# An unused tile of 416 bytes at the high end of SBUF

## The chip, the core and the metric

The kernel runs on one core of a Trainium2 chip. The metric is the device time of one execution in microseconds (us). The core has five engines with an instruction stream each: TensorE (PE in the profile, its weight loads PEld), VectorE (DVE), ScalarE (ACT), GpSimd (POOL) and SyncE (SP, which here issues most of the transfers), and 16 DMA engines. SBUF is the memory that the engines read their operands from: 128 partitions, and a tile has an address within the partition.

## The reference

A decoder trunk of two layers on one sequence of 1024 tokens, width 1024, 16 heads of 64, in float32:

```
layer 0: x = x + nsa_attention(rmsnorm(x))      # compressed, selected (top 8 blocks of 64) and window branch, gated
         x = x + swiglu(rmsnorm(x))             # (silu(a) * b) @ w_down, hidden width 2816
shared K/V = rmsnorm(x) @ kv_w                  # three dilation groups
layer 1: x = x + dilated_attention(rmsnorm(x))  # own queries, windows (128,1), (512,4), (2048,16)
         x = x + swiglu(rmsnorm(x))
return rmsnorm(x)
```

A table of 32 relative-position buckets x 16 heads is added to every attention logit.

## The kernel before

All of it is one function, `trunk`, which opens pools of tiles as it goes. A pool is opened on the left (low) or on the right (high) end of SBUF, and tiles of the two ends grow towards each other, so that a pool can be closed while one on the other end stays. The order of all instructions is fixed when the program is built; a tile that takes the memory of an earlier one waits until the earlier one's readers and writers are done.

**Products in three parts.** A float32 operand is split into a high part of type fp32r and the rest (`split`, L134 to L142; `Pairs`, L761 and L762: ACT copies the high part `ph`, DVE subtracts it and leaves `pl`). A product is then three matmuls (`mm3`, L165 to L167). The first operand is the stationary one, loaded as weights; the second moves through:

```
nc.tensor.matmul(ps, lh, rh, start=first, stop=False, ...)     # L165: high x high
nc.tensor.matmul(ps, lh, rl, start=False, stop=False, ...)     # L166: high x low
return nc.tensor.matmul(ps, ll, rh, start=False, stop=last, ...)  # L167: low x high
```

In the profile's names, `dx<-pl,ph` is a matmul into the bank dx with one operand from pl and one from ph; dx<-ph has both from ph tiles.

**The stages** of the profiled execution, in us from its start:

- 0 to 288: the projections of layer 0. The normalized, transposed stream (tiles hH, hL) and the weights (wraw, wh, wl) are all tiles of the right end; the bank is mm.
- 288 to 755: the attention of layer 0. Its pools are on the left, only its output oT on the right. SP loads the bias tiles T (L554) and the tiles K and V; POOL copies a part of each T into C (L561).
- 755 to 1505: output projection and FFN of layer 0.
- 1505 to 1927: K, V and the queries of layer 1, 18 groups of 128 output columns by the same routine as the FFN's first half.
- 1927 to 2245: the attention of layer 1.
- 2245 to 3036: output projection and FFN of layer 1.

**The big products** are by the scheme of seven block products in place of eight. `cols_steps` makes the hidden blocks (and the K, V and query blocks): its second operands are prepared once and kept for the stage, the tiles B11, B21, B22 and T1 to T4, and each of its seven steps is twelve matmuls of 128x512 with the weight's pair (ph, pl), sliced in four, as the stationary operand:

```
def blk(b, a, name, first, prev=None):
    for i in range(4):
        mm = mm3(b, part(a, i), ops[name][i], first and i == 0, i == 3, True)
```

Its banks are ux and uy (in the projections of layer 1 also dr). `rows_steps` makes the FFN's second half and the output projection; both its operands are pairs from one pool:

```
a, b = ready[i]
mm3(banks[t], part(a, t), b, i == 0 and onX != 2, i == n - 1, onX)
```

Its banks are dx and dr, and DVE adds them to the stream xr (L820). An FFN has 22 hidden blocks (`hidden`, each seven steps of `cols_steps`); after two of them come the seven steps of `rows_steps` (`down_steps`, 84 matmuls), put between the next two blocks' steps. So one period is 2 x 84 + 84 matmuls. The raw weights come into slices of the large tile oT (layer 0) or oTb (layer 1), and POOL multiplies them by the norm's gains (L1081).

**Where the tiles lie.** In the FFN of layer 0 the pairs ph, pl and the tiles wd, ta and tb are on the left, the B and T tiles, xr and oT on the right. In the projections of layer 1 the B and T tiles are on the right and the pairs on the left. In the FFN of layer 1 the pairs, wd, ta and tb are on the right, the B and T tiles, xr and oTb on the left. All these tiles have sizes that are multiples of 512 bytes. In the built program the right-hand ones begin at 480 modulo 512 bytes, the left-hand ones of the FFNs and of layer 1's projections at 64.

Of the kernel before, what the change touches and what calls it, by code (L numbers as in the profile page):

```python
# [10 lines left out]
F32 = mybir.dt.float32  # L11
# [80 lines left out]
def trunk(ctx, tc, I, out):  # L92
    nc = tc.nc

    def pool(c, name, side="left", space=None):
        if space is not None:
            return c.enter_context(tc.tile_pool(name=name, bufs=1, space=space,
                                                **({} if space is DR else {"reuse_waits": "tile"})))
        return c.enter_context(tc.tile_pool(name=name, bufs=1, side=side, reuse_waits="tile"))
# [17 lines left out]
        return psum[name].tile([128, 512], F32, name=name, bufs=BANKS.get(name, 1))  # L117

    cst = pool(ctx, "cst")

    ident = cst.tile([128, 128], F32, name="ident")
    nc.gpsimd.dma_start(ident, I["ident"])
# [1541 lines left out]
```

## Time and profile before

| | |
|---|---|
| median of 3 runs | 3033.9 us (3033.78 to 3038.08) |
| profiled execution, span | 3035.7 us |
| TensorE's mean granted clock | 0.983 |
| busy: PE, PEld | 2899.3 us, 2381.4 us |
| busy: DVE, ACT, POOL | 2401.7 us, 1603.6 us, 1630.1 us |
| moved by DMA | 293.43 MB |

The profile is of one execution. Busy times count instructions that do work; a matmul's record has a start, and an end that is modelled and overlaps the start of the next matmul, so the pace of matmuls is read from one start to the next. "The chain" is the work that ended last, followed back from the end of the program to whatever released each step. In a group's line the numbers behind the bar are its busy time in us, the mean of one in ns, and the idle time of the engine just before its instructions with what ended it. A window's line gives each engine's busy time and number of instructions, then the clock granted to TensorE, the mean busy share of the DMA engines and the GB/s.

### The profile page before, as it was taken

To read this page: it belongs to the slowest core of one execution; us is meant where nothing else is said; L and a number is where in the kernel's file an instruction comes from. 1 tells how busy PE (TensorE), PEld (TensorE's weight loads), DVE (VectorE), ACT (ScalarE), POOL (GpSimd) and SP (SyncE) were. 2 spreads that over 40 slices of the span, in tenths; PEclk is the share of its full clock that TensorE was granted. 3 is DMA by queue.
4 is the path that set the end of the run, shared out by engine and by line. 5 is a ranking of instruction groups with operands and counts; after the bars stand their busy time and mean duration, and the time that the engine had idled before them with its cause. 6 is when DMAs were issued, how large, how long until landed. Compare 5 with 4: busy or idle time off the path is not lost.

```text
span 3035.7 us, 44147 instructions
## 1 busy us (share of the span) xinstructions
PE 2899.3 (96%) x14670; PEld 2381.4 (78%) x14670; DVE 2401.7 (79%) x4832; ACT 1603.6 (53%) x3596; POOL 1630.1 (54%) x1751
## 2 busy tenths in 40 slices
PE   7999999999889999999999999899988899999997
PEld 6987888888677877777777778788866787777776
DVE  4432888988988888888876677589899788888887
ACT  5432888887463333333364444689965433333334
POOL 2134666666766555555556787333357755555551
PEclk9999999999999999999999999999999999999999
DMA  6765032121112222222124555876420211112111
GB/s 167 223 191 165 25 103 78 36 56 70 60 53 63 63 67 74 65 59 70 56 95 141 160 160 145 264 209 179 138 94 25 66 55 57 56 46 62 51 45 73
DMA packets 266196, 293.43 MB, mean 97 GB/s; under 512 B 17971, under 2 KB 209347, under 8 KB 265968
## 3 DMA queue, kind: packets, MB, share of 16 engines
q1 hardware_dynamic: 246320, 230.45, 26.3%
q0 software_dynamic: 19648, 60.16, 6.6%
q8 instruction: 116, 1.90, 0.3%
q14 instruction: 112, 0.92, 0.1%
HBM read 227.44 MB, written 78.81 MB: 101 GB/s over the span
## 4 chain that ended last, share of the span: by engine, by line
PE 68%; DVE 16%; ACT 5%; issue 4%; DMA 4%; POOL 2%; SPq 1%; DVEq 0%; ACTq 0%; POOLq 0%
PE ux L165 5%; PE ux L166 5%; PE ux L167 5%; PE uy L166 4%; PE uy L165 4%; PE uy L167 4%; DVE pl L762 4%; PE pt L275 4%; PE dx L166 3%; PE dr L165 3%; PE dx L167 3%; PE dx L165 3%; PE dr L166 3%; PE dr L167 3%; PE mm L165 3%
## 5 line engine op out<-in xcount | busy, mean ns | idle before, releaser
L762 DVE TENSOR_TENSOR pl<-oT,ph 128x512 fp32r<-128x512 f32 x315 | 325.2, 1052 | 41.3 <-ACT ph L761 35.4
L761 ACT ACTIVATE ph<-oT 128x512 fp32r<-128x512 f32 x329 | 199.0, 626 | 228.1 <-PE ux L166 65.8
L275 PE MATMUL pt<-ident,P 128*128 128x128 f32 x1536 | 245.1, 278 | 11.0 <-ACT P L1458 2.7
L761 ACT ACTIVATE ph<-oTb 128x512 fp32r<-128x512 f32 x239 | 143.2, 625 | 189.4 <-PE ux L166 55.7
L762 DVE TENSOR_TENSOR pl<-oTb,ph 128x512 fp32r<-128x512 f32 x229 | 224.4, 1005 | 23.5 <-ACT ph L761 23.4
L820 DVE TENSOR_TENSOR xr<-xr,dr 128x512 f32<-128x512 f32 x336 | 214.6, 679 | 33.9 <-PE dr L167 33.8
L139 DVE TENSOR_TENSOR tl<-pt,th 128x512 fp32r<-128x512 f32 (+1 forms) x320 | 207.1, 651 | 33.8 <-ACT th L138 31.9
L820 DVE TENSOR_TENSOR xr<-xr,dx 128x512 f32<-128x512 f32 x352 | 220.3, 678 | 3.6 <-PE dx L167 2.4
L166 PE MATMUL dx<-pl,ph 128*128 128x512 f32 x512 | 203.4, 401 | 9.7 <-DVE pl L762 9.0
L688 POOL TENSOR_SCALAR P<-P,sm,gates 128x384 f32<-128x384 f32 (+7 forms) x256 | 183.5, 728 | 53.4 <-DVE sm L686 48.0
L275 PEld LDWEIGHTS pt<-ident,P 128*128 128x128 f32 x1536 | 179.8, 142 | 30.0 <-ACT P L1458 6.7
L138 ACT ACTIVATE th<-pt 128x512 fp32r<-128x512 f32 (+1 forms) x320 | 177.2, 563 | 44.3 <-PE pt L275 40.4
L167 PE MATMUL dx<-ph,pl 128*128 128x512 f32 x512 | 200.0, 397 | 0.3 <-DVE pl L762 0.3
L684 ACT ACTIVATE P<-P,m 128x384 f32<-128x384 f32 (+7 forms) x256 | 170.7, 669 | 16.1 <-DVE m L682 8.4
L1081 POOL TENSOR_TENSOR oT<-oT,gffn 128x512 f32<-128x512 f32 x92 | 105.9, 1158 | 136.2 <-DMA oT<-in_ffn_w_up_dram 110.5
L165 PE MATMUL dx<-ph 128*128 128x512 f32 x512 | 157.3, 400 | 6.7 <-DVE xr L820 3.3
L1081 POOL TENSOR_TENSOR oTb<-oTb,gffn 128x512 f32<-128x512 f32 x92 | 106.4, 1165 | 99.1 <-DMA oTb<-in_ffn_w_up_dram 77.0
L298 PE MATMUL o<-tl,V 128*128 128x256 f32 x540 | 148.8, 299 | 7.4 <-POOL tl L291 3.7
L297 PE MATMUL o<-th,V 128*128 128x256 f32 x540 | 151.4, 296 | 2.7 <-ACT th L138 1.4
L290 POOL TENSOR_SCALAR th<-traw 128x128 fp32r<-128x128 f32 (+1 forms) x112 | 75.1, 674 | 129.3 <-ACT traw L289 47.7
L1458 ACT ACTIVATE P<-P,st 128x384 f32<-128x384 f32 (+2 forms) x256 | 139.6, 547 | 7.6 <-PE pt L1569 4.1
L166 PEld LDWEIGHTS dx<-pl,ph 128*128 128x128 f32 x512 | 97.6, 191 | 39.5 <-DVE pl L762 19.4
(617 smaller groups left out, 9582.4 us busy)
## 6 DMA issues: line engine op xcount, KB each, us to landing
qB<-xr POOLq DMA_DIRECT2D x96, 256.0 KB, 4.7
oT<-in_ffn_w_up_dram SPq DMA_DIRECT2D x92, 256.0 KB, 3.0
oTb<-in_ffn_w_up_dram SPq DMA_DIRECT2D x92, 256.0 KB, 3.0
Q<-qB SPq DMA_DIRECT2D x40, 512.0 KB, 7.0
wd<-in_ffn_w_down_dram SPq DMA_DIRECT2D x66, 256.0 KB, 2.6
oT<-in_b_w_q_dram SPq DMA_DIRECT2D x48, 256.0 KB, 3.5
K<-kBs SPq DMA_DIRECT2D x40, 256.0 KB, 9.5
wraw<-in_a_w_in_dram SPq DMA_DIRECT2D x18, 512.0 KB, 4.9
```

Source lines behind the costliest of these rows:

```text
L138: nc.scalar.activation(H_, src, AF.Copy)
L139: nc.vector.tensor_sub(L_, src, f32(H_))
L165: nc.tensor.matmul(ps, lh, rh, start=first, stop=False, skip_group_check=bool(shared))
L166: nc.tensor.matmul(ps, lh, rl, start=False, stop=False, skip_group_check=bool(shared))
L167: return nc.tensor.matmul(ps, ll, rh, start=False, stop=last, skip_group_check=bool(shared))
L275: nc.tensor.transpose(ps[:, i * 128:(i + 1) * 128], b, ident)
L684: nc.scalar.activation(P[:, e, :n], P[:, e, :n], AF.Exp, bias=mm[:, e:e + 1], scale=-1.0, accum_out=sm[:, e:e + 1])
L688: nc.gpsimd.tensor_scalar(P[:, e, :n], P[:, e, :n], sm[:, e:e + 1], gt(g, t, br, 2 * hp + e, 1), op0=OP.mult, op1=OP.mult)
L761: nc.scalar.activation(h, src, AF.Copy)
L762: (eng or nc.vector).tensor_sub(l, src, f32(h))
L820: nc.vector.tensor_add(xs, xs, banks[t])
L1081: nc.gpsimd.tensor_mul(v, v, gains[:, k:k + 4].unsqueeze(2).to_broadcast([128, 4, 128]))
```

## The change

A pool named "shift" is opened on the right, ahead of all others of that end, and one tile of 128 partitions x 104 floats (416 bytes in each partition) is taken from it. No instruction uses the tile.

```
     cst = pool(ctx, "cst")
+    pool(ctx, "shift", "right").tile([128, 104], F32, name="shift")
```

All 1114 tiles of the right end begin 416 bytes lower, at 64 modulo 512 bytes in place of 480; those of the left end stay. Every engine has the same instructions in the same order. What differs, beside addresses, is some waits at the places where a tile takes memory that others have left, since a shifted tile may overlap other ones than before. Lines below L119 have numbers higher by one, and tile numbers are higher by four.

The waits that differ are nearly all on SP where the attention of layer 0 begins (286 to 297 us). T8 to T11 are the first bias tiles for the first half of the tokens, K2, K3 and V2 the first keys and values; what the wait names is the semaphore (DMASW and DMAHW are transfers that POOL and SP have issued). Before:

```order
L554 DMA T8_2725<-sA_74 128x512 [waits DMAHW0_49]
L554 DMA T9_2732<-sA_74 128x512 [waits DMASW7_49,DMAHW1_49,DMASW0_49,DVE_49]
L554 DMA T10_2739<-sA_74 128x512 [waits DMASW4_49,DMAHW2_49,DMASW3_49,DVE_49]
L554 DMA T11_2746<-sA_74 128x512 [waits DMAHW3_49,DMASW2_49,DMASW1_49]
L267 DMA K2_2753<-kS_79 64x1024 [waits DMAHW4_49,DMASW6_49,DMASW5_49]
L268 DMA K2_2753<-kS_79 64x1024 [waits DMAHW5_49]
L569 DMA K3_2754<-kS_79 64x1024 [waits DMAHW6_49,PE_49]
L570 DMA K3_2754<-bS_81 16x1024 [waits DMAHW7_49]
L580 DMA V2_2759<-vS_80 128x4x128 [waits DMAHW0_49]
```

The same rows of SP after the change:

```order
L555 DMA T8_2729<-sA_78 128x512 [waits DMAHW0_49]
L555 DMA T9_2736<-sA_78 128x512 [waits DMASW4_49,DMASW7_49,DMASW3_49,DMAHW1_49,DMASW0_49,DVE_49]
L555 DMA T10_2743<-sA_78 128x512 [waits DMAHW2_49,DMASW2_49,DMASW1_49]
L555 DMA T11_2750<-sA_78 128x512 [waits DMAHW3_49,DMASW6_49,DMASW5_49]
L268 DMA K2_2757<-kS_83 64x1024 [waits DMAHW4_49]
L269 DMA K2_2757<-kS_83 64x1024 [waits DMAHW5_49]
L570 DMA K3_2758<-kS_83 64x1024 [waits DMAHW6_49,PE_49]
L571 DMA K3_2758<-bS_85 16x1024 [waits DMAHW7_49]
L581 DMA V2_2763<-vS_84 128x4x128 [waits DMAHW0_49,PE_49]
```

Each wait for POOL's stores has moved to the load one place ahead: T9 also waits for the two that T10 waited for, T10 for T11's, T11 for K2's, and K2 for none; V2 has a wait for a matmul of the stage before. In the attention of layer 1 one wait for PE has moved from the load of T126 to the one ahead of it, T125.

## The prediction

> **What bounds the kernel now.** I read the page first: the line of engines (the fraction of the span that each is busy) and the head of the chain that ended last (which engine's work, followed back from the end, fills the span).
>
> ```profile
> span 3035.7 us, 44147 instructions
> PE 2899.3 (96%) x14670; PEld 2381.4 (78%) x14670; DVE 2401.7 (79%) x4832; ACT 1603.6 (53%) x3596; POOL 1630.1 (54%) x1751
> PE 68%; DVE 16%; ACT 5%; issue 4%; DMA 4%; POOL 2%; SPq 1%; DVEq 0%; ACTq 0%; POOLq 0%
> ```
>
> TensorE (PE) is the bound, in busy time and in the chain. An average over stages can mislead, so next come stretches of single stages: the last projections of layer 0 (212 to 287), the FFN of layer 0 (900 to 1350), the K/V and query projections of layer 1 (1600 to 1905, and a part of them, 1816 to 1918), and the FFN of layer 1 (2400 to 2960).
>
> ```profile
> core 0: us, PE busy (x) PEld busy (x) DVE busy (x) ACT busy (x) POOL busy (x), PEclk, DMA share, GB/s
> 212.00:287.00 75.00, 75.00 (x332) 62.09 (x331) 12.81 (x18) 9.78 (x16) 33.57 (x72) 1.00 0.68 201
> 900.00:1350.00 450.00, 447.71 (x1909) 357.01 (x1908) 387.47 (x524) 168.11 (x289) 252.75 (x189) 1.00 0.26 68
> 1600.00:1905.00 305.00, 301.35 (x1296) 240.39 (x1295) 209.93 (x220) 142.15 (x223) 220.97 (x242) 1.00 0.52 151
> 1816.00:1918.00 102.00, 102.00 (x437) 81.97 (x436) 66.56 (x71) 47.17 (x71) 63.70 (x73) 1.00 0.57 169
> 2400.00:2960.00 560.00, 557.98 (x2375) 443.54 (x2374) 481.25 (x655) 207.32 (x356) 303.95 (x230) 1.00 0.18 53
> ```
>
> PE is full in all of them at a granted clock of 1.00, but the matmuls do not all come at one pace. 75 us hold some 331 of them, 226 to 227 ns each; 102 us hold some 436, 234 ns each. All are 128x512 fp32r matmuls. That asks for the timeline of PE, where two starts in a row give the pace.
>
> ```profile
> 211.96 0.39 PE L167 MATMUL mm<-hH,wl 128*128 128x512 f32 x1
> ...
> 287.47 0.39 PE L167 MATMUL mm<-hH,wl 128*128 128x512 f32 x1
> ...
> 1004.65 0.39 PE L166 MATMUL dx<-pl,ph 128*128 128x512 f32 x1
> ...
> 1006.23 0.39 PE L167 MATMUL dx<-ph,pl 128*128 128x512 f32 x1
> 1006.46 0.40 PE L165 MATMUL uy<-B21h,ph 128*128 128x512 f32 x1
> ...
> 1008.80 0.39 PE L166 MATMUL uy<-B21l,ph 128*128 128x512 f32 x1
> ...
> 1815.62 0.39 PE L166 MATMUL dr<-T1l,ph 128*128 128x512 f32 x1
> ...
> 1918.71 0.40 PE L167 MATMUL uy<-T3h,pl 128*128 128x512 f32 x1
> ```
>
> From 211.96 to 287.47 lie 333 steps without a gap: 75.51 / 333 = 226.8 ns. From 1815.62 to 1918.71 lie 440: 103.09 / 440 = 234.3 ns. In one stretch of the FFN, with the same neighbours on the other engines, the eight steps from 1004.65 to 1006.46 take 1.81 us (226 ns) and the ten from 1006.46 to 1008.80 take 2.34 us (234 ns). What divides them is where the two operands lie. hH, hL, wh and wl are all tiles of the right end, and in dx<-ph,pl both operands come from the pair tiles of one pool. In uy<-B21h,ph and dr<-T1l,ph the B and T tiles come from one end of SBUF and the pair tiles ph, pl from the other. In the built program the right-hand tiles begin at 480 modulo 512 bytes, the left-hand ones of these stages at 64. So, in this trace, a matmul whose stationary and moving operand begin at the same place modulo 512 runs at 226.8 ns when undisturbed, and one whose operands do not takes 7.5 ns more. No other difference that I tried (distance in bytes, side, layer, number of matmuls into one bank) sorts the groups.
>
> **The change, part by part.** (1) The unused tile itself: no instruction reads or writes it, every engine has the same instructions in the same order, so it costs 0. (2) The tiles of the right end move by 416 bytes, from 480 to 64 modulo 512, where the left ones of the dense stages lie. Which matmuls does that change from mixed to same? Those of `cols_steps`, seven steps of 12 matmuls: 22 x 84 = 1848 in each FFN, twice, and 18 x 84 = 1512 in the projections of layer 1; 5208 in all. The dx and dr matmuls, and the projections of layer 0, have both operands on one side and stay alike.
>
> What one is worth: the undisturbed ends give 234.3 - 226.8 = 7.5 ns. In the busy loop of an FFN I take less. Over both FFN stages, averaging steps under 320 ns in the timeline, ux and uy stand at 233.8 ns, dx, already alike, at 229.4 and dr at 231, since there the other engines are busy too (DVE 387.47 of 450 us). After the change I expect ux and uy to run as dx and dr do, nearest to dx, which also accumulates in a held bank: 233.8 - 229.4 = 4.4 ns. How much of it reaches the end shows in the loop's period, one recurring piece of the chain of waits in each FFN:
>
> ```profile
> 1184.94 2.39 DVE xr L820 x4
> 1244.20 2.39 DVE xr L820 x4
> ...
> 2615.36 2.39 DVE xr L820 x4
> 2674.63 2.39 DVE xr L820 x4
> 2733.95 2.39 DVE xr L820 x4
> ```
>
> A period of two hidden blocks is 59.3 us (1244.20 - 1184.94; 2674.63 - 2615.36) and holds 252 matmuls: 168 x 233.8 + 84 x 230 ns = 58.6 us, so PE accounts for all but 0.7 us of it. Hence 168 x 4.4 = 0.74 us less per period, 58.5 after, and 22 x 0.74 = 16.3 us in both layers. In the projections of layer 1 DVE is busy 66.56 of 102 us, between the clean stretch (12.81 of 75) and the FFN; I take 228 ns after, 234.3 - 228 = 6.3 ns x 1512 = 9.5 us. Sum 25.8 us of PE's time. PE is idle 2.3 of 450, 2.0 of 560 and 3.7 of 305 us in these stretches, so nearly all of it lies on the path; I let 90% through, as ends of steps wait for DVE and transfers: 23 us.
> Bounds: 5208 x 7.5 ns = 39 us if all reach 226.8, at 92% 36 us; below, dr's 231 in the FFN, 3696 x 2.8 = 10.3, with the projections at 231 also, 1512 x 3.3 = 5.0, and 60% through: 9 us.
>
> A rule of the Trainium skill speaks against this: "SBUF — State Buffer", section "Who interferes with whom", gives PE two independent read ports, one for the moving operand and one for the weight load, and says that PE never waits on anyone. By it the place of an operand would be no matter and the sum 0. The 226.8 and 234.3 ns of this trace do not fit that, unless something else parts them; that is the first rival.
>
> (3) Waits that change, since tiles now take memory that other tiles left: at the start of layer 0's attention SP's bias loads T9 and T10 wait for a store that T10 and T11 waited for before, and a load of K moves ahead. SP and POOL there:
>
> ```profile
> 286.58 6.69 SPq L554 DMA_DIRECT2D T<-sA  x3
> 293.70 0.71 SPq L267 DMA_DIRECT2D K<-kS  x1
> ...
> 301.90 0.51 POOL L558 TENSOR_SCALAR_AFFINE_SELECT TW<-T 128x384 f32<-128x384 f32 x1
> 302.35 0.23 POOL L561 COPY C<-T 128x32 f32<-128x32 f32 x1
> 302.70 0.40 POOL L561 COPY C<-T 128x32 f32<-128x32 f32 x2
> 303.71 0.23 POOL L561 COPY C<-T 128x32 f32<-128x32 f32 x1
> ...
> T<-sA SPq DMA_DIRECT2D x32, 256.0 KB, 4.4
> ```
>
> The whole queue is through with T by 293.3, at the latest the time for T9; it lands at the median of 4.4 us by 297.7, and its copy comes at 302.70. What hides it is the first attention blocks' own work: 5 us in hand. Were the landing 10 us, 0.6 us would be lost. Behind T9 stand only K and V on SP, needed later still. Cost 0. In layer 1, one T load takes a PE wait from the next one that is over 20 us old: 0.
> (4) Matmuls of 128x256 in the attentions, o<-th,V above all: layer 0's are left-side on both operands and stay; in layer 1 some 384 have operands on both sides, at unlike places before and after. The 256-wide matmuls of the first stages start 117 to 120 ns apart, the alike ones no faster than the others: 384 x 3 ns, about 1 us of either sign; I take 0.
> (5) DVE, ACT, POOL and transfers: do they feel the place?
>
> ```profile
> oT<-in_ffn_w_up_dram SPq DMA_DIRECT2D x92, 256.0 KB, 3.0
> oTb<-in_ffn_w_up_dram SPq DMA_DIRECT2D x92, 256.0 KB, 3.0
> L762 DVE TENSOR_TENSOR pl<-oT,ph 128x512 fp32r<-128x512 f32 x315 | 325.2, 1052 | 41.3 <-ACT ph L761 35.4
> L762 DVE TENSOR_TENSOR pl<-wd,ph 128x512 fp32r<-128x512 f32 x86 | 78.9, 919 | 3.1 <-ACT ph L761 3.1
> L762 DVE TENSOR_TENSOR pl<-tb,ph 128x512 fp32r<-128x512 f32 x56 | 69.1, 1234 | 40.3 <-ACT ph L761 40.3
> L762 DVE TENSOR_TENSOR pl<-ta,ph 128x512 fp32r<-128x512 f32 x56 | 55.2, 985 | 12.7 <-ACT ph L761 12.6
> ```
>
> A weight load lands in 3.0 us on either side. pl<-oT,ph reads tiles of both ends, pl from wd, ta and tb those of one end: 919, 985 and 1234 ns lie around the 1052. Place does not order them, and I take 0.
>
> The profiled execution took 3035.7 us, 1.8 above the median of 3033.9; the saving is the same against either. 3033.9 - 23 = 3011 us.
>
> **The rivals.** (a) *The place is not the cause.* cols_steps differs from the others in more than its sides: it always streams a prepared block past four slices of a pair. Then every matmul keeps its pace and the time stays 3034. For it speaks only that I have no stretch of cols_steps with both operands on one side; against it, that dx<-pl,ph has the same slices and the same banks' length of accumulation.
> (b) *DVE takes over.* It is busy 387.47 of 450 us, 51 of each period of 59.3. At a period of 58.5 it stands at 87%, so it is no bound by sum, but a pair pl that comes late stops PE. If half of the 25.8 us comes back so, 13 us remain: 3021.
> (c) *Slower: DVE's two SBUF reads collide.* Now oT or oTb lies like ph and pl. If those 544 operations (315 + 229) went from about 1032 to the 1234 ns of pl<-tb, +20%, and PE gained nothing, it would cost what they hold of the chain: pl's share there is
>
> ```profile
> by line: PE ux L165 5.5%; PE ux L166 5.4%; PE ux L167 5.3%; PE uy L166 4.3%; PE uy L165 4.3%; PE uy L167 4.3%; DVE pl L762 4.1%; issue 4.0%; PE pt L275 3.8%; PE dx L166 3.0%; PE dr L165 2.8%; PE dx L167 2.8%; PE dx L165 2.8%; PE dr L166 2.7
> ```
>
> 4.1% or 124 us, two thirds of it theirs, 83 us x 20% = 16 us: 3050. With PE's gain of 23 us it decides from +28% on. Against it: wd at 919 and ta at 985 already lie so.
>
> **How the numbers follow.** Forecast (2999 to 3017 us) 0.69; (b), 3017 to 3028, 0.13; (a) 0.12; (c) 0.06. The range 2999 to 3028 takes in the first two. A measurement of this kernel can tell some 0.2%, 6 us (the three runs lie 4.3 us apart), so: faster 0.82, same 0.12, slower 0.06.
>
> **What would show it.** In the changed profile the run of matmuls that now goes from 1815.62 to 1918.71 has steps near 228 ns instead of 234.3; the period of the FFN falls from 59.3 to about 58.5 us; the steps at 211.96 to 287.47 stay at 226.8; DVE's mean for pl<-oT stays near 1052; POOL's first copy of T does not wait. The forecast is wrong if ux and uy keep 234 ns (a), or go to 227 while the period stays (b).

## The result, and the profile after

The changed kernel takes 3015.0 us (median of 6 runs, 3012.0 to 3022.8) against 3038.7 us for the kernel before, run beside it (6 runs, 3033.8 to 3046.4): a ratio of 0.9924 with a 95% interval of 0.9908 to 0.9939. That is 23 us of 3034. 3011 were forecast, 23 us below the 3033.9 of the page before. The profiled execution took 3014.1 us, its span is 3012.3.

The head of the page, and the engines' shares of the chain that ended last:

```profile
span 3012.3 us, 44147 instructions
PE 2869.0 (95%) x14670; PEld 2378.2 (79%) x14670; DVE 2405.6 (80%) x4832; ACT 1600.7 (53%) x3596; POOL 1640.1 (54%) x1751
PE 61%; DVE 22%; ACT 6%; issue 5%; DMA 3%; POOL 2%; SPq 1%; DVEq 0%; ACTq 0%; POOLq 0%
```

PE's busy time fell by 30 us, the other engines' hardly moved. In the chain PE went from 68 to 61% and DVE from 16 to 22%: PE still bounds, but DVE is now last more often. In PE's timeline, the same matmuls as in the prediction (dx into uy<-B21, and the start of the run that was 1815.62 to 1918.71 before):

```profile
998.80 0.39 PE L168 MATMUL dx<-ph,pl 128*128 128x512 f32 x1
...
999.93 0.39 PE L166 MATMUL uy<-B21h,ph 128*128 128x512 f32 x1
...
1002.20 0.39 PE L167 MATMUL uy<-B21l,ph 128*128 128x512 f32 x1
...
1802.00 0.39 PE L167 MATMUL dr<-T1l,ph 128*128 128x512 f32 x1
...
1903.60 0.39 PE L168 MATMUL uy<-T3h,pl 128*128 128x512 f32 x1
```

The five steps up to 999.93 take 1.13 us (226 ns), the ten after it 2.27 us (227 ns, 234 before): the step in pace between dx and uy is gone. The long run takes 101.60 us in place of 103.09. 440 steps at 226.7 ns would be 99.7 us; the rest is six longer steps, the longest 1.1 us, which were not there before.

Both traces hold the same 14670 matmuls in the same order, so they can be laid on each other. I split the steps from one start to the next into pace (under 320 ns in both) and gaps (the others), and take the differences by stage (755 to 1505, 1505 to 1927 and from 2245 on in the trace before; matmuls of other widths count in the last two columns only):

```
                          pace of the 512-wide    gaps     all steps of the stage
FFN and output, layer 0        -14.0 us         +6.8 us          -7.0 us
projections of layer 1          -9.8            +7.1             -3.3
FFN and output, layer 1        -14.6            +5.3             -9.1
elsewhere                       -0.1            -2.5             -3.7
sum                            -38.5           +16.6            -23.1
```

So the pace gave 38 us, and 16 to 17 of these came back as gaps. In the projections of layer 1 the gaps of different executions differ by as much: three later kernels in which little pace was won there, or none, had 5.1, 7.7 and -0.4 us more gaps than the profile before. What was lost there is not put down to the change. The 12 us in the two FFNs are: other profiles with the full pace and all of DVE's work (416 bytes on the left, 160 bytes, the changed kernel once more, all below) have 9.5, 13.5 and 15.1 us more gaps there than before, and that with 32 bytes, at a fifth of the pace gain, 3.0. The stretch of one FFN in the windows, and a recurring piece of the chain in each FFN, which give the period:

```profile
core 0: us, PE busy (x) PEld busy (x) DVE busy (x) ACT busy (x) POOL busy (x), PEclk, DMA share, GB/s
900.00:1350.00 450.00, 445.96 (x1934) 360.67 (x1933) 397.50 (x531) 169.52 (x292) 256.18 (x188) 1.00 0.26 67
...
1222.81 2.98 DVE pl L763 x2
1280.93 2.61 DVE pl L763 x2
...
2586.13 2.98 DVE pl L763 x2
2702.41 2.99 DVE pl L763 x2
2818.67 2.99 DVE pl L763 x2
```

The period is 58.1 us in both (1280.93 - 1222.81; 2702.41 - 2586.13 is two of them): 58.5 was forecast from 59.3, and 252 matmuls at 227 ns alone would be 57.2. PE's idle time in the stretch rose from 2.3 to 4.0 us, and DVE's share from 86 to 88%.

The moved waits of SP, and DVE's subtractions:

```profile
290.95 2.35 SPq L555 DMA_DIRECT2D T<-sA  x3
...
301.83 0.41 POOL L562 COPY C<-T 128x32 f32<-128x32 f32 x2
...
L763 DVE TENSOR_TENSOR pl<-oT,ph 128x512 fp32r<-128x512 f32 x315 | 333.7, 1079 | 40.8 <-ACT ph L762 34.6
```

T9 is issued at 290.95 in place of 286.58, its copy comes at 301.83 without an idle time ahead of it: hidden. pl<-oT, whose operands now begin at one place, takes 1079 ns, 1052 before. The subtractions from ta and tb, whose operands began at one place before as well, went from 985 to 1096 and from 1234 to 1118 ns, so a few per cent here say nothing of the place.

### The profile page after: what moved, and what is told of

It reads as the page before. It is cut to its first block, busy times and chain, and to the rows that moved or that the text cites. A ratio compares the mean times of both kernels' runs of the same rounds, so it can differ in the third digit from the quotient of the medians.

```text
span 3012.3 us, 44147 instructions
## 1 busy us (share of the span) xinstructions
PE 2869.0 (95%) x14670; PEld 2378.2 (79%) x14670; DVE 2405.6 (80%) x4832; ACT 1600.7 (53%) x3596; POOL 1640.1 (54%) x1751
## 4 chain that ended last, share of the span: by engine, by line
PE 61%; DVE 22%; ACT 6%; issue 5%; DMA 3%; POOL 2%; SPq 1%; DVEq 0%; ACTq 0%; POOLq 0%
DVE pl L763 7%; PE ux L166 5%; DVE xr L821 5%; PE ux L167 5%; PE ux L168 4%; PE pt L276 4%; PE uy L166 4%; PE uy L167 4%; PE uy L168 4%; PE dx L167 3%; PE mm L166 3%; PE dx L168 3%; PE mm L167 3%; PE mm L168 2%; PE dr L166 2%
## 5 line engine op out<-in xcount | busy, mean ns | idle before, releaser
L763 DVE TENSOR_TENSOR pl<-oT,ph 128x512 fp32r<-128x512 f32 x315 | 333.7, 1079 | 40.8 <-ACT ph L762 34.6
L762 ACT ACTIVATE ph<-oT 128x512 fp32r<-128x512 f32 x329 | 198.8, 626 | 222.3 <-PE ux L167 58.5
```

The lines of the kernel that those rows point to most:

```text
L762: nc.scalar.activation(h, src, AF.Copy)
L763: (eng or nc.vector).tensor_sub(l, src, f32(h))
```

## The experiments

There were three theories at first. Theory 1: the pace of a matmul is set by how its two operands' places differ. Theory 2: 480 is a bad place by itself, being no multiple of 64. Theory 3: the gain came from the moved waits (beside the seven on SP that are listed with the change, six on POOL differ). The ratios below are to the kernel before, run beside each.

**Another size of the unused tile, 32 bytes.**

```
+    pool(ctx, "shift", "right").tile([128, 8], F32, name="shift")
```

> The unused tile has 32 bytes in place of 416: the right-hand tiles begin at 448 modulo 512, a multiple of 64 as the left-hand 64 is, but not at the same place. Theory 1 (the pace of a matmul is set by the difference of its two operands' places modulo 512): ux and uy keep some 234 ns from start to start, the dr and dx right behind them 228 to 232, and the time stays within 0.2% of before. Theory 2 (what hurts is that 480 is no multiple of 64, and 416 bytes mend that): ux and uy go to 227 ns and the time falls by 0.8%, as with 416 bytes. Theory 3 (the gain of 416 bytes came from moved waits): any time, with ux and uy at 234 ns.

Measured: 0.998 (0.9968 to 0.9992), 6 us less. The pace gain was 7.3 us in all, with ux and uy at 232.8 ns in the FFNs: a small gain and not the 38 us of 416 bytes. All waits of this program are those of the kernel before.

**The unused tile at the other end.**

```
+    pool(ctx, "shift").tile([128, 104], F32, name="shift")
```

> The unused tile of 416 bytes is taken from the left end instead: the tiles of both ends begin at 480 modulo 512, the same place, and no multiple of 64; the right-hand tiles stay where they were before. Theory 1 (difference of the operands' places): ux, uy, dx and dr all at 227 ns, the time 0.6 to 0.9% below before. Theory 2 (480 is a bad place, being no multiple of 64): ux and uy at 234 ns or more, and the time the same as before or above it. Theory 3 (moved waits): the waits of this kernel are others than those of the change, so no gain, at 234 ns.

Measured: 0.9928 (0.9911 to 0.9944), as the change itself. The ten steps of uy<-B21 in PE's timeline, of the kernel with 32 bytes on the right:

```profile
1003.35 0.40 PE L166 MATMUL uy<-B21h,ph 128*128 128x512 f32 x1
...
1005.68 0.40 PE L167 MATMUL uy<-B21l,ph 128*128 128x512 f32 x1
```

and of the kernel with 416 bytes on the left:

```profile
1001.09 0.39 PE L166 MATMUL uy<-B21h,ph 128*128 128x512 f32 x1
...
1003.36 0.39 PE L167 MATMUL uy<-B21l,ph 128*128 128x512 f32 x1
```

The ten steps take 2.33 us against 2.27 us: 233 and 227 ns. With all places multiples of 64 but different the pace is slow; with all at 480 and alike it is fast. Theory 2 falls. Theory 3 isn't tested by this run, against what I had expected of it: since the two ends move towards each other by the same 416 bytes, the waits that differ are those of the change here too.

**160 bytes, half of 512 apart.**

```
+    pool(ctx, "shift", "right").tile([128, 40], F32, name="shift")
```

> The unused tile has 160 bytes: the right-hand tiles begin at 320 modulo 512, the left-hand ones at 64, so they differ by 256. Theory 1 with a period of 512 bytes: ux and uy stay near 234 ns, time as before within 0.2%. Theory 1 with a period of 256 bytes (or a part of it): 227 ns and 0.8% less, as with 416 bytes. Theory 2 (only multiples of 64 matter): 227 ns and 0.8% less. A pace between the two would say that the cost grows with the difference.

Measured: 0.9914 (0.9897 to 0.9931), pace gain 38.0 us, uy<-B21 at 226.7 ns. So the operands need not begin at the same place modulo 512: **256 is the period**. This was open in the expectation, and the prediction's 512 is too strict. Theory 2 allowed this result, but has fallen already. Theory 3 falls here: T9 to V2 have the waits of the kernel before in this program, and the gain is there. The wait that moves from T126 to T125, and two on POOL, do differ; the program with 352 bytes further down has the same ones, and gains 9 us where this one gains 26.

**The matmul by itself.** A small kernel with runs of 48 matmuls, stationary slices 512 bytes apart, moving slices 2048 bytes apart:

```
a = s // 4 + i % 4 * 128
nc.tensor.matmul(b, st[:, a:a + 128], mv[:, m // 4 + i % 3 * 512:m // 4 + i % 3 * 512 + 512], ...)
```

> Leaves out the whole decoder and writes a placeholder: 48 matmuls of 128x512 fp32r in a row for each of 17 places of the moving operand against the stationary one (0 to 480 bytes on), five pairs of absolute places, and four times 24 at a difference of 416 followed by 24 at 0; the other engines are idle. Theory 1: 226.8 ns at difference 0 whatever the absolute place, up to 234 ns at most others (416 and 96, the two of the kernel, for certain), and after 24 at 416 the first three to nine at 0 are still off 226.8. Theory 2: multiples of 64 all at 226.8, 16, 32 and 480 slower, and the pair at 32 and 32 slower too. Theory 3, or a cause in the other engines: all at 226.8 ns.

PE's timeline, stretches within the runs at differences 0, 64, 256 and 416 (the last number is the count; start, and time to the end of the last one, which is 0.39 us behind its start):

```profile
27.76 9.46 PE L39 MATMUL g<-mv,st 128*128 128x512 f32 x41
...
61.65 9.09 PE L39 MATMUL g<-mv,st 128*128 128x512 f32 x39
...
128.21 9.00 PE L39 MATMUL g<-mv,st 128*128 128x512 f32 x39
...
183.72 9.53 PE L39 MATMUL g<-mv,st 128*128 128x512 f32 x40
```

(9.46 - 0.39) / 40 = 226.8 ns, 228.9, 226.6 and 234.4 ns. Over the last half of each run, by the place of the moving operand minus that of the stationary one:

```
difference, bytes     0      16     32     64     96     128    160    192    224
ns per matmul       226.7  231.7  233.3  228.9  233.3  233.3  234.2  233.3  233.3
256 bytes further   226.7    -    233.3  228.9  233.3  233.3  234.2  233.3  233.3
```

(16 bytes was tried only once.) Both operands at 32, or both at 416, ran at 226.7 too once settled, and three pairs at a difference of 96 from other places at 233.3: the absolute place plays no part, and no other engine is needed. The kernel's own differences are 416 (160 modulo 256; 234.2) where the pairs are on the left, and 96 (233.3) where they are on the right. The difference has a sign, since 64 and 192 are not alike. And a run at one difference carries into the next: behind 24 matmuls at 416, steps at difference 0 read 235, 232, 231, 227, 226, 227, and elsewhere 230, 236, 229, 232, 231 before they settle. The runs of 24 were partly reordered when the program was built, so the settling was read at seven seams into a run at difference 0, with two to ten steps each. At two of these seams the run ahead was at difference 0 too, with both operands at another place (from 0 to 416, and back): nine steps were off at each, so here a change of place alone disturbed the pace for a while. By the map, 32 bytes on the right (128 modulo 256 in all stages) should have given 0.9 ns where the pairs are on the left, some 3 us of the 7.3 found; the 2.8 us that were won in layer 1's FFN it does not explain.

**352 bytes, to try that map on the whole kernel.**

```
+    pool(ctx, "shift", "right").tile([128, 88], F32, name="shift")
```

> The unused tile has 352 bytes: right-hand tiles begin at 128 modulo 512, left-hand ones at 64. In layer 0's FFN and in the projections of layer 1 the moving operand then lies 64 behind the stationary one, in layer 1's FFN 64 ahead (192 modulo 256). By the map of the small kernel (228.9 ns at 64, 233.3 at 192) the three stages part: ux and uy at 229 to 230 ns in layer 0's FFN and in the projections, 233 to 234 in layer 1's FFN; some 17 us of pace, of which 55 to 65% reach the end: 8 to 13 us below before. If only the size of the difference counted, both FFNs would have one pace; if only equal places helped, none would gain.

Measured: 0.997 (0.9957 to 0.9982), 9 us; pace gain 6.1 us in layer 0's FFN stage, 7.3 in the projections of layer 1, 1.6 in layer 1's FFN stage. ux and uy stood at 230.0 ns in layer 0's FFN and 233.6 in layer 1's. The map tells the stages apart, with its sign.

**Where the rest of the pace went.** Theory A: DVE comes late when PE is faster. Theory B: the gaps have nothing to do with DVE. First half of one kind of DVE's work is left out, in the kernel before and in the changed one:

```
-    xs = xr[:, 4 * r + t, c * 512:(c + 1) * 512]
-    nc.vector.tensor_add(xs, xs, banks[t])
+    xs = xr[:, 4 * r + t, c * 512:c * 512 + 256]
+    nc.vector.tensor_add(xs, xs, banks[t][:, :256])
```

> The kernel before, with half of VectorE's additions into the stream left out: each add of a product to xr takes 256 of 512 columns, in the output projections and the FFNs. VectorE then has some 0.3 us less to do 31 times in each period of the FFN. Beside the next run it tells where the pace gain of the change went (38 us less from start to start, 15 to 17 us more in steps over 320 ns). Theory A (VectorE comes late once PE is faster): before the change VectorE was seldom the last, so this kernel is 0 to 10 us faster than before. Theory B (the lost part sits in waits that have nothing to do with VectorE's load): the same as before within 5 us.

Measured: 0.9961 (0.9947 to 0.9975), 12 us less, a little more than expected.

> The changed kernel with the same half of VectorE's additions left out. Theory A: against the run before this one it is 30 to 36 us faster, since in the FFNs the pace gain now goes through whole (some 28 us of pace there, 10 in the projections of layer 1, less the 5 to 7 us of longer gaps there, which this edit does not touch); its gaps over 320 ns in the FFNs are no longer than those of the run before this one. Theory B: against it 23 us faster as with all the additions, with the gaps some 10 us longer in the FFNs.

Measured: 0.9847 (0.9825 to 0.9868). Against the run with less work before it that is 0.9886 (0.986 to 0.991, from the two intervals), 35 us, where the change on the whole kernel gave 23. Laid on each other, these two have 29.6 us of pace between them in the two FFN stages and 1.6 us fewer gaps, where the whole kernels have 28.6 and 12.1 us more. By line, the chain of the kernel before in layer 1's FFN (2400 to 2960):

```profile
by line: PE ux L165 12.1%; PE ux L167 11.8%; PE ux L166 11.7%; PE uy L167 8.6%; PE uy L166 8.6%; PE uy L165 8.5%; PE dx L166 6.0%; PE dx L167 5.6%; PE dx L165 5.3%; PE dr L165 4.4%; PE dr L166 4.2%; PE dr L167 4.1%; DVE xr L820 3.8%; DVE pl
```

that of the changed kernel (2400 to 2940):

```profile
by line: PE ux L166 10.7%; PE ux L167 10.3%; PE ux L168 10.1%; DVE xr L821 9.6%; DVE pl L763 8.4%; PE uy L166 6.9%; PE uy L167 6.9%; PE uy L168 6.8%; PE dx L167 5.1%; PE dx L168 4.6%; PE dx L166 3.4%; issue 3.4%; PE dr L166 3.4%; PE dr L167
```

and that of the changed kernel with half of the additions left out (2400 to 2900):

```profile
by line: PE ux L166 12.8%; PE ux L167 12.7%; PE ux L168 12.7%; PE uy L167 9.7%; PE uy L168 9.7%; PE uy L166 9.6%; PE dx L166 6.3%; PE dx L167 6.3%; PE dx L168 6.3%; PE dr L168 4.7%; PE dr L166 4.6%; PE dr L167 4.6%
```

DVE's additions to xr have 3.8% of the chain in the first and 9.6% in the second, where its subtractions (pl) have another 8.4%; in the third DVE has none. Theory B falls.

DVE's lateness does not always show as PE waiting for DVE. In the changed kernel, rows around the first T2 step in one period of layer 0's FFN:

```profile
1001.00 1.67 POOL L1005 TENSOR_TENSOR oT<-oT 128x512 f32<-128x512 f32 x1 [7.01 <-DVE pl L763]
...
1002.71 1.15 ACT L762 ACTIVATE ph<-oT 128x512 fp32r<-128x512 f32 x2 [2.11 <-POOL oT L1005]
...
1003.39 0.19 PEld L166 LDWEIGHTS ux<-T2h,ph 128*128 128x128 f32 x1 [0.43 <-ACT ph L762]
```

PE's weight load waits for ACT's copy, which waits for GpSimd, which waited for DVE. In the FFN stages 32 steps into the T2 matmuls take over 320 ns after the change, where 4 did before; what they take beyond 227 ns grew by 5.6 us, nearly half of the 12.1. With half of the additions left out none is that long.

**Less for DVE without leaving work out.** In the changed kernel, the low parts of two weight blocks go to GpSimd in all hidden blocks:

```
-    eng=nc.gpsimd if j < 3 else None)
+    eng=nc.gpsimd)
```

> The changed kernel with the low parts of the first two weight blocks of every hidden block subtracted by GpSimd in place of VectorE (the code does so for the first three hidden blocks; here for all 22). VectorE has four operations of about 1.05 us less in a period of 58 us, GpSimd four of about 1.2 us more, of some 33 that it is busy. Theory A: part of the 10 us of gaps in the FFNs is won back, 3 to 8 us below the change. Theory B, or if GpSimd's reads hold up VectorE's other subtractions: the same as the change or up to 15 us above it.

Measured: 0.989 (0.987 to 0.9909), some 10 us below the changed kernel, the best of theory A's forecast and somewhat beyond it. The gaps in the two FFN stages fell by 15 us against the changed kernel's, and the long steps into T2 from 32 to 4; in this one profile layer 0's attention took 8.6 us more and gave part of it back. The same edit on the kernel before:

> The kernel before (no unused tile), with GpSimd in place of VectorE for the same four subtractions per period as in the run on the changed kernel. Theory A (VectorE's lateness, made worse by a faster TensorE): here less is to be won than the 10 us on the changed kernel, 2 to 8 us, as matmuls at 234 ns leave VectorE more time. Theory C (the four operations are worth the same whatever TensorE's pace, so they say nothing of where the change's gain went): 10 us here too, and the change is worth 23 us on top of either version.

Measured: 0.9986 (0.9976 to 0.9995), 4 us. So the edit is worth 4 us at the old pace and about 10 at the new one, and the change is worth 0.989 / 0.9986 = 0.9904 (0.988 to 0.993), 29 us, where GpSimd takes that load. By these times alone theory C isn't excluded, since 23 us lie inside that interval (21 to 36 us). The traces speak against it: at the old pace the edit leaves the gaps of the FFN stages as they were (0.7 us more), at the new one it takes out 15 us; and between the two kernels with the edit the FFN stages have 29.0 us of pace and 2.3 us fewer gaps.

A third block for GpSimd, in the changed kernel:

> The changed kernel with a third weight block's subtraction on GpSimd as well (that of step m7), six operations per period. VectorE falls by another 2 of 58 us, GpSimd rises from some 39 to 41. If VectorE's lateness still costs something, 1 to 4 us below the version with four; if that is spent, or GpSimd's longer operation now comes late itself, the same as it or some us above.

Measured: 0.9889 (0.9874 to 0.9903): no different from the version with four.

And the changed kernel again:

> The changed kernel once more, beside the two others on one chip: 0.991 to 0.994 of before.

Measured: 0.9938 (0.9923 to 0.9952). In this execution the gaps in the FFN stages are 15.1 us longer than before, and the pace gain is 38.4 us: the account repeats.

The fastest version that leaves nothing out is the change with the GpSimd edit, 0.989 of before with four operations moved and 0.9889 with six; the latter is 0.9889 / 0.9938 = 0.9951 (0.993 to 0.997) of the changed kernel run beside it.

## Why the prediction came out right

*The cause.* The forecast rested on the place of a matmul's two operands, read from 226.8 against 234.3 ns. That is shown: by the left-hand tile, by 160 bytes, and by the matmuls alone. Rival (a), another cause with no gain, falls. By the Trainium skill, "SBUF — State Buffer", section "Who interferes with whom", PE reads the moving operand and the weights through two independent ports. If that is taken to mean that the place does not matter, these runs do not agree: 226.7 against 234.2 ns by the place alone. What in the engine makes the place count, no run here shows. "The same place modulo 512" was too narrow: modulo 256 is enough.

*The size per matmul.* Here the working failed. I took 4.4 ns for ux and uy in the FFNs, since dx and dr, already alike, ran at 229.4 and 231 ns, and put that down to other engines being busy. But dx and dr were slowed by the unlike matmuls ahead of them: they stood at 228.0 and 227.1 to 227.4 after the change, with DVE as busy as ever. In layer 1's FFN, a run of twelve dx that read 233, 236, 224, 231, 236, 228, 232, 231, 227, 227, 226 ns from start to start (at 2436.7 before) has only 226 and 227 after. So ux and uy went from 233.8 to 227.1, 6.7 ns, and dx and dr gained as well: 28.6 us of pace in the two FFN stages, where 16.3 was forecast. In the projections of layer 1 the term held: 9.8 us against 9.5.

*What reaches the end.* I let 90% through. Of 38.5 us it was 23, 60%: the FFNs kept 16 of 28.6 us. The two errors, a pace gain too small and a loss too small, cancel nearly to the microsecond, and that is luck: the place was understood, the size of the saving was not. Rival (b) had the mechanism of the loss, a pair that comes late while DVE's sum of 87% is no bound, and half of the gain lost; 40% was. I gave it 0.13. In these runs DVE, busy for 88% of the stretch, kept PE waiting for one late operation at a time, directly or through GpSimd and ACT.

*The period* fell to 58.1 us, 58.5 forecast, by the same two errors.

*The rest held.* The waits for T were hidden; pl<-oT rose by 2.6%, not 20%, so rival (c) falls; the projections of layer 0 stayed at their pace. The attention stages moved by -3.9 and +1.0 us in this pair, as they do between executions.

## What to carry to other kernels

Read the pace of back-to-back matmuls from start to start, and sort it by where the two operands begin modulo 256 bytes; tiles from two ends of SBUF may differ there, and an unused tile set it right here, of 416 or of 160 bytes. When a group looks slowed by its surroundings, look first at what ran just ahead of it on the same engine. And price a gain on a saturated engine against the next engine piece by piece: DVE's 88% of the time did not mean that its pieces came in time.

## What the runs showed of the hardware

A 128x512 fp32r matmul, back to back with others, takes 226.7 ns when its moving and stationary operand begin at the same place modulo 256 bytes, and between 228.9 (moving 64 bytes on) and 234.2 ns (160 bytes on) when they do not, whatever their absolute place and with the other engines idle. The wrong pace lasts for up to ten matmuls beyond the ones that cause it, and at two seams a change of place alone, from one run at difference 0 to another, left nine off. Other types and widths were not tried.
